# Branch projections: where the low parts of the streamed weights are computed, VectorE or GpSimd

## The chip, the cores and the metric

One core of a Trainium2 chip runs the whole program. The metric is the device time of one execution in microseconds (us), the median of several. TensorE, VectorE, ScalarE and GpSimd stand in the profile as PE, DVE, ACT and POOL, the queue that issues most transfers as SP; PEld is TensorE's loading of weights.

## The reference

One block of a transformer on 1024 tokens of width 1024, float32 throughout. Cut to what matters here:

```python
u = x * (1.0 + scale1) + shift1
proj = u @ w_in                       # 4808 columns: a_q a_k a_v b_q b_kv i_q i_k i_w gates
y_a = diff_attention(a_q, a_k, a_v)   # 4 heads x 2 maps, block-causal, ALiBi
score = sum_h i_w * relu(i_q . i_k)   # the indexer; the 256 best keys of a row are selected
o_lat = attention over the selected keys of c_kv, 8 heads
y_b = o_lat @ w_uv
mixed = sigmoid(gates_a) * (y_a @ w_a_proj) + sigmoid(gates_b) * (y_b @ w_b_proj)
x = layer_norm(alpha * x + gate1 * (mixed @ w_o))
# then 16 experts, two of them for each token, and a second layer norm
```

## The kernel before

Each float32 matrix that TensorE multiplies is split into a high part, the value rounded by ScalarE (`copy` in `halves`, L132), and a low part, the value less the high part (`sub`, L128). A product is then three matmuls, low by high, high by low and high by high (`mm3`, lines L142, L145, L146).

The streamed weights of the projections come in chunks of 128 columns: two transfers of 128x512 into `raw` (tag `wr`, two buffers), two copies into `wh` by ScalarE, two subtractions into `wl`. `wh` and `wl` have two buffers each, so the chunk after next is converted while TensorE works at the next. A chunk is 48 matmuls into `pj`. There are 34 chunks that go this way through `wload`: one of the indexer, one of `kv`, 12 of branch A, 4 of the queries of B, 16 of gates. `merge_a` multiplies the output of branch A by its merge weights, eight chunks of 128x512, which are split in the same way into halves of a `wab` buffer. Branch B's merge weights (`load_wab`), `w_o` and the experts' weights are split by the same function.

Two streams are woven by the generators' own numbers: `attentions` (scores of the indexer, the top-k search on VectorE, attention A, attention B) and `fillers` (`kv`, `b_keys`, gates, projections of A and B, `a_norm`, `merge_a`). The scheduler of the language then puts the instructions of each engine into one order by a model of their times; each engine, and each queue of transfers, works through its own order, and an instruction that waits holds everything behind it.

Names that the prediction uses. `ptr`, `pth`, `ptl`: the transposed probabilities and their two parts, which TensorE needs for `py` (attention A) and `pyb` (attention B). `plg`: logits, which VectorE takes out of PSUM as `P` at L762 and L778. `macc`: a sum over rows of the conditioning weights `adaw`, which VectorE makes in the middle of the projections (L694) from transfers of 512 KB, for values that are first needed behind the attentions; `gb` is read back from it. `yo` and `yq`: the output of attention A and its clipped copy (L900). `mask_d`: the masks that the top-k search ends in, stored from GpSimd's queue (L600) out of VectorE's `e` (L598). `bqq`, `bqh`, `bql`, `bv`: loads for a head of attention B, issued from GpSimd's queue (L263, L924). GpSimd does no arithmetic on tiles in this kernel: it fills constants, stores and loads.

Of the kernel before, what the change touches and what calls it, by code (L numbers as in the profile page):

```python
# [86 lines left out]
def block_kernel(ctx: ExitStack, tc, a, out):  # L87
    nc = tc.nc
    V, S, G, PE = nc.vector, nc.scalar, nc.gpsimd, nc.tensor
# [40 lines left out]
    def copy(o, i, e=None):  # L130
        if e is None:
            return S.activation(o, i, AF.Copy)  # L132
        return e.tensor_copy(o, i)
# [60 lines left out]
    def after(i, name):  # L194

        if name:
            tc.add_manual_dep(i.ins, name, mybir.DependencyInfo(mybir.DependencyClass.NoSync, mybir.DependencyReason.DATA),
                              reason="order of two streams")

    def halves(src, h, l, split, queue=dma, behind=None, tag="wr", raws=None, times=None):  # L200

        if raws is None:
            raws = fetch(src, h.shape[1], queue, tag)
        for c, raw in raws:
            cs = slice(c, c + raw.shape[1])
            if times is not None:
                V.tensor_tensor(raw, raw, times[:, cs], op=OP.mult)
            after(copy(h[:, cs], raw), behind)
            sub(l[:, cs], raw, h[:, cs], split)
        return h, l  # L210

    def fetch(src, n, queue, tag):
        w = 512 if tag in HALVES else 1024
        raws = []
        for c in range(0, n, w):
            raw = (s2 if tag in HALVES else s4)("raw", tag)[:, :min(w, n - c)]
            queue(raw, src[:, c:min(c + w, n)])
            raws.append((c, raw))
        return raws

    def wload(src, n=1024, split=V):
        return halves(src, s4("wh", "wh", dt=FR)[:, :n], s4("wl", "wl", dt=FR)[:, :n], split)

    def proj(ch, use, split=V, w=None, tag="mm"):

        h, l = w or wload(a["w_main"][ch], split=split)
        for half in range(2):
            p = bank("pj", tag)
            t = slice(half * 512, half * 512 + 512)
            for k in range(KC):  # L230
                c = slice(k * 128, k * 128 + 128)
                mm3(p, h[:, c], l[:, c], uh[k][:, t], ul[k][:, t], k == 0, k == KC - 1, True)
                if k % 2 and k < KC - 1:
                    yield 1.3
            use(half, p)
            for side, n in sides:
                for _ in range(n):
                    next(side, None)
            yield 1.3
# [83 lines left out]
    for n in range(3):  # L323
        tag = ("lg", "lg", "mm")[n]
# [700 lines left out]
    def merge_a():  # L1025
        for c in range(KC):
            w = s4("wab", ("wh", "wl")[c % 2], (128, 2, 512), FR)
            wh, wl = halves(a["w_ab"][c, :, 0:512], w[:, 0], w[:, 1], V, S.dma_start)
            for half in range(2):
                t = slice(half * 512, half * 512 + 512)  # L1030
                g = s2("gate", "sg")
                dma(g, gates_d[c, :, t])
                p = bank("pab", "mm")
                for k in range(4):
                    cs = slice(k * 128, k * 128 + 128)
                    mm3(p, wh[:, cs], wl[:, cs], yah[k][:, t], yal[k][:, t], k == 0, k == 3, True)
                    yield 2.5
                V.tensor_tensor(g, p, g, op=OP.mult)
                dma(gates_d[c, :, t], g)
# [71 lines left out]
    for c in range(KC):  # L1111
        wh, wl = wab.pop(0) if wab else load_wab(c)
# [719 lines left out]
```

## Time and profile before

| | us |
|---|---|
| median of 3 runs | 1384.12 (1382.36 to 1387.14) |
| the profiled execution | 1381.05 |
| its span, first to last instruction | 1379.2 |
| PE busy | 1255.9 (91%) |
| DVE busy | 977.6 (71%) |
| ACT busy | 682.6 (49%) |
| POOL busy | 122.4 (9%) |
[...]

The profiled execution took 1.85 us more than its span and lies 3.07 us under the median of the runs. Busy time is the union of an engine's instructions; matmuls overlap, so a stretch in which PE is busy all the time still has a pace of its own. Until about 640 us the projections run beside the top-k search and attention A, then attention B beside the merge of A until about 870 us; the output product, the routing and the experts follow, and the last norm ends the program.

### The profile page before, as it was taken

How to read it: one execution, taken by the hardware profiler on the slowest of the kernel's cores; microseconds unless marked ns; L12 is line 12 of the kernel's file. 1: busy time of each engine (PE TensorE's matmuls, PEld its weight loads, DVE VectorE, ACT ScalarE, POOL GpSimd, SP SyncE). 2: the span in 40 equal slices, each digit the busy share in tenths (PEclk: the TensorE clock that was granted, in tenths of full speed). 3: DMA queues.
4: the chain of work that ended last, by engine and by line, in shares of the span. 5: the costliest groups of instructions: out<-in, count | busy, mean ns of one | idle time of the engine just before them, and what ended most of it. 6: DMA issues, size and time to landing. Idle time of an engine off the chain costs nothing. (4 is left out here: it accounts for less than half of the span.)

```text
span 1379.2 us, 18485 instructions
## 1 busy us (share of the span) xinstructions
PE 1255.9 (91%) x6280; PEld 988.6 (72%) x6295; DVE 977.6 (71%) x2128; ACT 682.6 (49%) x1214; POOL 122.4 (9%) x154
## 2 busy tenths in 40 slices
PE   7999999999999999998889988899986989999950
PEld 6876778877777777666667777787865767788840
DVE  6547689783457758665676768888798889877736
ACT  4536662213785555445746556434224557554515
POOL 1000000000000001001001100000002222323120
PEclk9999999999999999999999998999996999999985
DMA  9211442123124317564445521675435788989856
GB/s 362 80 46 70 145 174 86 47 67 121 53 82 145 130 54 237 177 191 129 142 146 145 160 79 61 222 242 190 156 128 208 237 298 249 311 290 310 244 87 249
DMA packets 108485, 225.90 MB, mean 164 GB/s; under 512 B 33104, under 2 KB 39648, under 8 KB 108384
## 3 DMA queue, kind: packets, MB, share of 16 engines
q1 hardware_dynamic: 67952, 164.22, 33.8%
q0 software_dynamic: 35824, 52.03, 14.0%
q10 hardware_dynamic: 4608, 8.39, 1.9%
q8 instruction: 53, 0.87, 0.2%
q14 instruction: 48, 0.39, 0.1%
HBM read 169.94 MB, written 54.58 MB: 163 GB/s over the span
## 5 line engine op out<-in xcount | busy, mean ns | idle before, releaser
L142 PE MATMUL pj<-uh,wl 128*128 128x512 f32 x544 | 220.7, 406 | 1.6 <-ACT bkr L132 0.8
L145 PE MATMUL pj<-ul,wh 128*128 128x512 f32 x544 | 216.5, 398 | 0.0
L146 PE MATMUL pj<-uh,wh 128*128 128x512 f32 x544 | 215.9, 397 | 0.0
L128 DVE TENSOR_TENSOR ewl<-raw,ewh 128x1024 fp32r<-128x1024 f32 x102 | 122.2, 1218 | 28.6 <-ACT ewh L132 28.6
L132 ACT ACTIVATE ewh<-raw 128x1024 fp32r<-128x1024 f32 x102 | 105.6, 1057 | 61.5 <-DMA raw<-w_exp 61.0
L142 PEld LDWEIGHTS pj<-uh,wl 128*128 128x128 f32 x544 | 102.7, 189 | 35.1 <-issue 11.5
L146 PEld LDWEIGHTS pj<-uh,wh 128*128 128x128 f32 x544 | 102.5, 188 | 26.1 <-issue 5.6
L145 PEld LDWEIGHTS pj<-ul,wh 128*128 128x128 f32 x544 | 102.7, 189 | 23.6 <-issue 5.1
L132 ACT ACTIVATE pth<-ptr 128x512 fp32r<-128x512 f32 (+1 forms) x120 | 65.8, 552 | 70.8 <-PE ptr L793 39.0
L128 DVE TENSOR_TENSOR ptl<-ptr,pth 128x512 fp32r<-128x512 f32 (+1 forms) x120 | 75.4, 634 | 23.6 <-ACT pth L132 22.8
L142 PE MATMUL pgu<-ewh,xl 128*128 128x512 f32 x200 | 81.3, 407 | 0.0
L793 PE MATMUL ptr<-ident,P 128*128 128x128 f32 x432 | 72.8, 286 | 7.7 <-DVE ptl L128 6.4
L145 PE MATMUL pgu<-ewl,xh 128*128 128x512 f32 x200 | 79.0, 395 | 0.0
L146 PE MATMUL pgu<-ewh,xh 128*128 128x512 f32 x200 | 79.0, 395 | 0.0
L765 ACT ACTIVATE P<-P,mx 128x128 f32<-128x128 f32 (+7 forms) x64 | 49.4, 772 | 41.5 <-DVE mx L762 37.5
L1612 POOL DMA_INDIRECT acc_d<-ot,idxs x24 | 47.3, 1969 | 201.1 <-DVE ot L1611 133.0
L793 PEld LDWEIGHTS ptr<-ident,P 128*128 128x128 f32 x432 | 52.3, 147 | 15.9 <-DVE ptl L128 7.9
L128 DVE TENSOR_TENSOR wl<-raw,wh 128x512 fp32r<-128x512 f32 x68 | 44.9, 686 | 22.9 <-ACT wh L132 22.8
L780 ACT ACTIVATE P<-P,mx 128x128 f32<-128x128 f32 (+3 forms) x64 | 49.4, 773 | 21.7 <-DVE mx L778 20.4
L758 PE MATMUL plg<-ak,aq 64*128 64x512 f32 (+4 forms) x288 | 58.2, 375 | 0.6 <-DVE mx L762 0.6
L444 DVE SCALAR_TENSOR_TENSOR sc<-relu,iw,sc 128x512 f32<-128x512 f32 (+3 forms) x70 | 45.4, 653 | 17.9 <-ACT relu L439 16.0
L958 PE MATMUL pyb<-ptl,bv 128*128 128x256 f32 (+1 forms) x160 | 47.8, 322 | 7.1 <-DVE ptl L128 3.7
(443 smaller groups left out, 2966.6 us busy)
## 6 DMA issues: line engine op xcount, KB each, us to landing
raw<-w_exp SPq DMA_DIRECT2D x102, 512.0 KB
raw<-w_main SPq DMA_DIRECT2D x68, 256.0 KB
adaw<-ada_b SPq DMA_DIRECT2D x32, 512.0 KB
adaw<-ada_a SPq DMA_DIRECT2D x16, 512.0 KB
gates_d<-gt SPq DMA_DIRECT2D x32, 256.0 KB
gate<-gates_d SPq DMA_DIRECT2D x32, 256.0 KB
xt<-xT SPq DMA_DIRECT2D x8, 512.0 KB
bv_d<-bvs SPq DMA_DIRECT2D x16, 256.0 KB
```

What stands on the lines that cost most here:

```text
L128: e.tensor_tensor(o, i0, i1, op=OP.subtract)
L132: return S.activation(o, i, AF.Copy)
L142: i = PE.matmul(o, wl, xh, start=first, stop=False)
L145: PE.matmul(o, wh, xl, start=False, stop=False)
L146: e = PE.matmul(o, wh, xh, start=False, stop=last)
L444: V.scalar_tensor_tensor(acc, r[:, :n], w, acc, op0=OP.mult, op1=OP.add)
L758: i = PE.matmul(p[:, :n], q[a_][r, qs], k[b_][r, c0:c0 + n], start=m == 0, stop=m == 2)
L765: S.activation(P[:, :L], P[:, :L], AF.Exp, bias=mx_[:, 0:1], scale=-1.0, accum_out=mx_[:, 1:2])
L780: S.activation(P[:, :L], P[:, :L], AF.Exp, bias=mx[:, 0:1], scale=-1.0, accum_out=mx[:, 1:2])
L793: leads(PE.transpose(p[:, c:c + 128], Ps[s][:, kb * 128:kb * 128 + 128], ident))
L958: PE.matmul(y[:, c0:c0 + n], st, tl, start=kb == 0, stop=False)
L1612: where(cond_p and cond_p(), lambda: G.indirect_dma_start(out=acc_d, out_offset=bass.IndirectOffsetOnAxis(ap=isc, axis=0), in_=ot, in_offs ...
```

## The change

`wload` and `proj` take GpSimd as the engine of the subtraction unless told otherwise, and `merge_a` names it. High parts stay on ScalarE. `load_wab`, `load_wo`, the first four chunks and the experts name VectorE as before.

```diff
-    def wload(src, n=1024, split=V):
+    def wload(src, n=1024, split=G):
         return halves(src, s4("wh", "wh", dt=FR)[:, :n], s4("wl", "wl", dt=FR)[:, :n], split)
 
-    def proj(ch, use, split=V, w=None, tag="mm"):
+    def proj(ch, use, split=G, w=None, tag="mm"):
...
     def merge_a():
         for c in range(KC):
             w = s4("wab", ("wh", "wl")[c % 2], (128, 2, 512), FR)
-            wh, wl = halves(a["w_ab"][c, :, 0:512], w[:, 0], w[:, 1], V, S.dma_start)
+            wh, wl = halves(a["w_ab"][c, :, 0:512], w[:, 0], w[:, 1], G, S.dma_start)
```

That is 68 subtractions of 128x512 for the 34 chunks and 8 for `merge_a`. The scheduler orders all engines anew. Three places show it.

POOL, from the end of the constants to the first loads for attention B; `wl` rows are the moved subtractions, two for a chunk, and the six `mask_d` stores are the end of the top-k search. A line with + stands in the changed program alone.

```order
 L395 IOTA dtmp 128x1024
+L128 TENSOR_TENSOR wl<-raw,wh 128x512 x28
 L559 UNCONDITIONAL_BRANCH
+L128 TENSOR_TENSOR wl<-raw,wh 128x512 x2
 L600 DMA mask_d<-e_2973 128x384
 L600 DMA mask_d<-e_2995 128x512
 L600 DMA mask_d<-e_3018 128x640
+L128 TENSOR_TENSOR wl<-raw,wh 128x512 x2
 L600 DMA mask_d<-e_3056 128x768
 L600 DMA mask_d<-e_3092 128x896
 L747 MEMSET bias 64x64 x2
 L600 DMA mask_d<-e_3147 128x1024
```

Behind these rows come the two subtractions of the 17th chunk: they now stand behind the last mask store, and those of the 16th behind the third.

DVE, at the end of attention A, the last three sums over `adaw` and the first parts `ptl` of the transposed probabilities behind them. Before:

```order
L694 SCALAR_TENSOR_TENSOR macc_5785<-adaw_6197,cond_68,macc_5785 128x1024
L947 RECIPROCAL rden_711<-mx_6041 128x1
L947 RECIPROCAL rden_711<-mx_6100 128x1
L694 SCALAR_TENSOR_TENSOR macc_5785<-adaw_6200,cond_68,macc_5785 128x1024
L694 SCALAR_TENSOR_TENSOR macc_5785<-adaw_6325,cond_68,macc_5785 128x1024
L1146 TENSOR_SCALAR gb_9192<-gb_9192 128x8
L128 TENSOR_TENSOR ptl_5879<-ptr_5874,pth_5878 128x384
L128 TENSOR_TENSOR ptl_5997<-ptr_5991,pth_5996 128x512
L251 SCALAR_TENSOR_TENSOR hl_6192<-pj_6092,hl_6191 128x512
```

The same place in the changed program:

```order
L128 TENSOR_TENSOR ptl_5879<-ptr_5874,pth_5878 128x384
L947 RECIPROCAL rden_711<-mx_6100 128x1
L128 TENSOR_TENSOR ptl_5997<-ptr_5991,pth_5996 128x512
L694 SCALAR_TENSOR_TENSOR macc_5785<-adaw_6197,cond_68,macc_5785 128x1024
L1146 TENSOR_SCALAR gb_9192<-gb_9192 128x8
L694 SCALAR_TENSOR_TENSOR macc_5785<-adaw_6200,cond_68,macc_5785 128x1024
L251 SCALAR_TENSOR_TENSOR hl_6192<-pj_6092,hl_6191 128x512
L694 SCALAR_TENSOR_TENSOR macc_5785<-adaw_6325,cond_68,macc_5785 128x1024
L900 TENSOR_SCALAR yq_5957<-yo_5954 128x256
L128 TENSOR_TENSOR ptl_6012<-ptr_6006,pth_6011 128x512
```

Two `ptl` have moved ahead of the three sums; `yq_5957` and `ptl_6012` stay behind them. ACT at the same time, before, where `raw` waits for a buffer that a `wl` subtraction frees:

```order
L132 ACTIVATE wh_6468<-raw_6472 128x512
L217 DMA raw_6917<-w_ab 128x512
L217 DMA raw_7083<-w_ab 128x512
L132 ACTIVATE yo_5954<-py_5833 128x256
L132 ACTIVATE pth_6011<-ptr_6006 128x512
```

And in the changed program:

```order
L132 ACTIVATE wh_6468<-raw_6472 128x512
L132 ACTIVATE yo_5954<-py_5833 128x256
L132 ACTIVATE pth_6011<-ptr_6006 128x512
L901 ACTIVATE yq_5957<-yq_5957 128x256
L217 DMA raw_6917<-w_ab 128x512
L217 DMA raw_7083<-w_ab 128x512
```

The two transfers have moved behind `yo`, `pth` and `yq`.

DVE, early in attention B, the third and fourth chunk of `merge_a` ahead of two reads of logits. Before:

```order
L128 TENSOR_TENSOR ptl_6389<-ptr_6383,pth_6388 128x512
L128 TENSOR_TENSOR wab_7486<-raw_7487,wab_7486 128x512
L128 TENSOR_TENSOR wab_7296<-raw_7297,wab_7296 128x512
L778 ISA P_6501,mx_6502<-plg_6503,bias_6352 128x512
L778 ISA mx_6502 128x1
L778 ISA P_6516,mx_6517<-plg_6518,bias_6352 128x320
```

The same place in the changed program:

```order
L128 TENSOR_TENSOR ptl_6389<-ptr_6383,pth_6388 128x512
L778 ISA P_6501,mx_6502<-plg_6503,bias_6352 128x512
L778 ISA mx_6502 128x1
L778 ISA P_6516,mx_6517<-plg_6518,bias_6352 128x320
L778 ISA mx_6517 128x1
```

The two `wab` rows are gone from DVE; TensorE's order at this place is the same in both programs.

## Rows read from the trace of the kernel before

**Rows 1.** The page: busy time of an engine, its share, instructions.

```profile
PE 1255.9 (91%) x6280; PEld 988.6 (72%) x6295; DVE 977.6 (71%) x2128; ACT 682.6 (49%) x1214; POOL 122.4 (9%) x154
```

**Rows 2.** Windows: stretch, length, busy us of PE, PEld, DVE, ACT, POOL; clock; DMA.

```profile
68.00:540.00 472.00, 469.42 (x2263) 356.65 (x2261) 317.87 (x755) 239.63 (x450) 6.16 (x14) 1.00 0.29 100
187.00:316.00 129.00, 127.49 (x564) 103.36 (x563) 110.52 (x257) 35.14 (x64) 3.79 (x8) 1.00 0.28 96
540.00:640.00 100.00, 93.83 (x471) 68.66 (x470) 61.31 (x151) 45.33 (x94) 6.82 (x10) 0.97 0.61 181
640.00:815.00 175.00, 158.72 (x898) 124.07 (x909) 119.43 (x329) 106.93 (x213) 15.81 (x26) 0.97 0.48 140
815.00:935.00 120.00, 109.36 (x547) 88.56 (x548) 96.89 (x202) 54.58 (x103) 0.82 (x2) 0.96 0.50 168
```

**Rows 3.** Line L128's subtractions and L444: shortest, median, longest ns; first, last start.

```profile
L128 DVE TENSOR_TENSOR wl<-raw,wh x68: 667/685/694, 67.7 to 625.5; 128x512 fp32r<-128x512 f32 x68
L128 DVE TENSOR_TENSOR wab<-raw,wab x16: 662/684/693, 641.3 to 895.5; 128x512 fp32r<-128x512 f32 x16
L444 DVE SCALAR_TENSOR_TENSOR sc<-relu,iw,sc x70: 467/671/753, 88.2 to 189.0; 128x512 f32<-128x512 f32 x35, 128x384 f32<-128x384 f32 x14, 128x320 f32<-128x320 f32 x14, 128x256 f32<-128x256 f32 x7
```

**Rows 4.** Groups on POOL: count, busy us, mean ns, idle before.

```profile
L1423 POOL MEMSET zt<- 128x512 f32 x1 | 0.5, 540 | 6.9 <-DVE mxl L128 6.9
L395 POOL IOTA dtmp<- 128x1024 f32 x1 | 1.0, 994 | 28.5 <-DVE mod L351 28.5
```

**Rows 5.** Timeline by engine, 291 to 316 us: start, duration, instruction, idle before.

```profile
299.81 0.69 DVE L128 TENSOR_TENSOR wl<-raw,wh 128x512 fp32r<-128x512 f32 x1
300.19 0.54 POOL L600 DMA_DIRECT2D mask_d<-e  x1 [4.60 <-DVE e L598]
303.03 0.39 PE L142 MATMUL pj<-uh,wl 128*128 128x512 f32 x1
305.14 0.63 ACT L132 ACTIVATE wh<-raw 128x512 fp32r<-128x512 f32 x1 [0.79 <-DMA raw<-w_main]
314.44 0.50 PE L142 MATMUL pj<-uh,wl 128*128 128x512 f32 x1 [0.36 <-ACT gt L720]
314.89 0.54 POOL L600 DMA_DIRECT2D mask_d<-e  x1 [0.78 <-DVE e L598]
```

**Rows 6.** Timeline by engine, 619 to 628 us.

```profile
619.14 1.28 DVE L694 SCALAR_TENSOR_TENSOR macc<-adaw,cond,macc 128x1024 f32<-128x1024 f32 x1 [4.32 <-DMA adaw<-ada_b]
621.98 1.28 DVE L694 SCALAR_TENSOR_TENSOR macc<-adaw,cond,macc 128x1024 f32<-128x1024 f32 x1 [1.56 <-DMA adaw<-ada_b]
623.26 1.15 DVE L128 TENSOR_TENSOR ptl<-ptr,pth 128x384 fp32r<-128x384 f32 x2
623.86 0.58 PE L145 MATMUL py<-ptl,avh 128*128 128x256 f32 x1 [4.72 <-DVE ptl L128]
625.63 1.05 ACTq L217 DMA_DIRECT2D raw<-w_ab  x2
626.79 0.38 ACT L132 ACTIVATE yo<-py 128x256 f32<-128x256 f32 x1 [10.20 <-DVE wl L128]
627.21 0.29 DVE L900 TENSOR_SCALAR yq<-yo 128x256 f32<-128x256 f32 x1 [1.00 <-ACT yo L132]
```

**Rows 7.** Timeline by engine, 667 to 670 us.

```profile
667.75 0.97 ACT L132 ACTIVATE pth<-ptr 128x512 fp32r<-128x512 f32 x2
667.89 0.69 DVE L128 TENSOR_TENSOR wab<-raw,wab 128x512 fp32r<-128x512 f32 x1 [1.73 <-ACT wab L132]
668.50 0.68 DVE L778 CUSTOM_DVE_ANT_0 P<-plg,bias 128x512 f32<-128x512 f32 x1
669.24 0.79 PE L774 MATMUL plg<-bql,bqq 128*128 128x512 f32 x1 [2.31 <-DVE mx L778]
```

**Rows 8.** Windows, with the granted clock behind the six busy columns.

```profile
621.40:628.20 6.80, 4.34 (x15) 3.85 (x16) 5.02 (x9) 1.39 (x4) 0.70 (x2) 0.50 0.74 217
669.10:672.50 3.40, 3.26 (x11) 2.55 (x13) 2.19 (x9) 2.90 (x5) 0.00 (x0) 0.51 0.49 158
```

## Prediction

> **What bounds the kernel now.** I read the page first: TensorE is busy for 91% of the span, VectorE for 71%, GpSimd for 9% [rows 1]. An average over stages decides nothing, so the windows come next [rows 2]. Between 68 and 540 us, where 30 of the 34 projection chunks are converted and the whole top-k search lies, TensorE is busy 469.4 of 472.0 us at the full granted clock. Every microsecond that VectorE gains there is worth nothing, unless TensorE waits for VectorE, and it does not. From 540 on TensorE idles: 6.2 us up to 640, 16.3 us up to 815 and 10.6 us up to 935, 33 us in all, and the clock falls below 1.00. Only there can work taken off VectorE shorten the program. So the question is which of those waits end at one of the moved instructions, or at something queued behind one.
>
> **What is moved.** 68 subtractions `wl` at 685 ns (46.6 us) and the first 8 of the 16 `wab` rows at 684 ns (5.5 us) leave VectorE [rows 3]. The same 76 go to GpSimd, which so far does no such instruction in this trace. Its price p has to be bounded: below by the fill of a tile of the same 128x512, 0.54 us, one pass that only writes; above by three such passes one after the other, two reads and a write, 1.6 us [rows 4]. I take two passes, 1.1 us, because two operands must come in. [...]
>
> **Term 1, the slower subtraction itself: 0.** Each chunk's `wl` is needed when TensorE has finished the chunk before it, and the double buffer leaves time. The shortest two gaps of the 34 are those of the 16th and 17th chunk: the 16th is ready at 300.50 and first used at 303.03, 2.5 us later [rows 5]; all but these two have 5 us or more. Two subtractions cost 2.2 us in place of 1.4 us, 0.8 us more; at 1.6 us, 1.9 us more. Both fit even into the 2.5 us. And those two chunks are late today only because VectorE is in the top-k search: ScalarE had done its half of the 17th at 305.8, 8.7 us ahead of the first use at 314.44 [rows 5]. If that cover were gone, each chunk that comes late costs TensorE what it is late by.
>
> **Term 2, GpSimd's queue: 0, with a condition.** GpSimd now holds the two subtractions of the 17th chunk behind the last mask store, which was issued at 314.89, after the first use of that chunk at 314.44 [rows 5]. Were VectorE no faster than today, the chunk would be ready at 314.89 + 0.54 + 2 x 1.1 = 317.6 and TensorE would wait 3.2 us. But VectorE is busy 110.5 of 129 us between 187 and 316 [rows 2], and 22 of the moved subtractions lie in that stretch ahead of the last store, 15 us by 685 ns each. If the search gains more than 3.2 of those 15 us, the wait is nil. I take nil. The loads and fills for attention B behind other `wl` rows in that queue wait for TensorE anyway, and the subtractions ahead of them have their data by then.
>
> **Term 3, the wait at 619 us: -4 us.** Here VectorE stood behind three sums `macc` whose transfers came late (4.32 us and 1.56 us of waiting in the two that are shown); the `ptl` that TensorE needed came behind them at 623.26, and TensorE idled 4.72 us [rows 6]. ScalarE was held too, for 10.2 us, since its transfer of `w_ab` waited for a `wl` on VectorE behind the same sums. In the new order two `ptl` stand ahead of the sums, and ScalarE's `yo` and `pth` ahead of that transfer. What still stands behind the sums is `yq` and the next `ptl`. With transfers as late as now, the last sum ends at 623.26; 0.29 us for `yq` and 0.69 us for `ptl` give 624.2. TensorE gets there later than 619.1: from the first `ptl` on it has 37 matmuls to do, and it reaches that `ptl` 15 matmuls earlier, both counted in TensorE's new order. At the mean pace of 68 to 540 us (472 us for 2263 matmuls, 0.21 us each [rows 2]) that is 619.1 - 3.2 + 7.8 = 623.7; many of the 37 are half as wide, so it may be 622. The wait left is 0.5 to 2.2 us, and 2.5 to 4.2 us are gained, 3.3 in the middle. Behind the wait the clock stood at half for 6.8 us, of which some 4.3 us were worked in, so 2.2 us were lost to it [rows 8]; a wait of half the length may still cost the shorter fall of 3.4 us [rows 8]. I add 0.7 us.
>
> **Term 4, the wait at 669 us: -2.5 us.** VectorE waits 1.73 us for ScalarE's half of a `wab`, subtracts for 0.69 us, and only then reads the logits at 668.50; TensorE, which needs that PSUM bank, idles 2.31 us [rows 7]. In the new order VectorE goes from a `ptl` straight to the logits. The next `ptl` still needs ScalarE's `pth` of 667.75, so some 1.1 us of the wait may come back one step later. The gain is 1.2 to 2.3 us, and 3.4 us at half clock behind it, worth 1.7 us [rows 8], may go. Between 1.2 and 4.0 I take 2.5.
>
> **Term 5, the other six `wab` subtractions, 717 to 761 us: -0.5 us.** They stand among `ptl` rows at 0.6 to 0.7 us each, and no wait of TensorE over 0.5 us follows one directly.
>
> **The sum.** 0 + 0 - 4 - 2.5 - 0.5 = -7 us. The profiled execution took 1381.05 us, so 1374 us in its measure; it lies 3.07 us under the median of the runs, so **1377 us** as a median, 0.5% less.
>
> **Rivals.** *A. Nothing to see.* All orders are new from the first scores on, and 33 us of small waits on long chains behind 540 us can come out elsewhere: what `yq` loses behind `macc`, for example, is the same 4.72 us one step on if the transfers land 3 us later. Against it speaks that TensorE's order in attention B is unchanged where term 4 lies. It gives 1381 to 1387 us.
>
> *B. Slower, through VectorE being held up.* If a VectorE instruction that takes both inputs from SBUF could not run beside a GpSimd subtraction, VectorE would pay for what it gave away. The indexer's sums (70 at some 0.67 us, 88 to 189 us [rows 3]) and the end of the search are of this kind, while `ptl` and the logits take one input from PSUM. The place is the last mask store, the price is that of the 17th chunk. With 22 subtractions of 1.1 us each holding VectorE fully, 24.2 us come back for the 15 us saved; the last store falls to about 324, the chunk is ready at 326.9, and TensorE waits 12.4 us in place of none, plus some 2 us of clock. Less the 7 us above, that is +7: 1391 us. TensorE begins to wait when VectorE loses more than 11.8 of its 15 us; from 18.8 us on the wait outweighs the gains. For it speaks that VectorE is nearly full in that stretch [rows 2]; against it that most of the search's time is one-input counting. [...] No row of the trace shows it, since GpSimd reads no tile so far; at full strength in that stretch it would make the 1391 us.
>
> *C. More than forecast.* VectorE's relief shortens further links of attention B's chain: a third of the 33 us of idling in place of the fifth or so above, with its clock: 1370 us.
>
> **Chances.** Forecast 0.43, C 0.13, A 0.28, B 0.16. 0.3%, about what a measurement of this kernel tells from no change, is 4.2 us. Forecast and C are faster, but the forecast's near end (-4) is not: faster 0.54, same 0.29, slower 0.17. The range takes in C and part of B, from 1368 to 1389 us. Its low end is C with 2 us to spare, its high end B less the last 2 us; the forecast alone would be 1373 to 1381.
>
> **What would show it.** Right: POOL subtractions at about 1.1 us; TensorE still full from 68 to 540 us; first uses of the 16th and 17th chunk without a wait; the idle 4.72 us at 619 cut to 2 us or less; the 2.31 us at 669 cut to about 1 us; the chain from 935 us on as before, only earlier. Wrong: TensorE waiting for `wl` on POOL at about 314 us, or VectorE instructions of L444 and L594 to L597 longer than now (B); the same sum of TensorE's idle time behind 540 us in other places (A). A price of 4 us or more on GpSimd would break term 1 in the whole search.

## The result, and the profile after the change

The changed kernel is slower. Its median is 1396.0 us (1391.7 to 1403.0, 8 runs), beside 1384.6 us (1375.3 to 1393.6, 8 runs) for the kernel before: a ratio of 1.010, 95% interval 1.0072 to 1.0128. Timed once more beside other kernels it gave 1.0077 (1.0048 to 1.0106). The profiled execution took 1393.96 us, 12.9 us more than that of before, and its span is 1391.9 us, at a mean granted clock of TensorE of 0.955 (0.958 before).

The page's first part (busy time of an engine, its share of the span, instructions), against [rows 1]:

```profile
PE 1259.5 (90%) x6280; PEld 992.2 (71%) x6295; DVE 958.2 (69%) x2052; ACT 680.3 (49%) x1214; POOL 225.2 (16%) x230
```

GpSimd took on 102.8 us of work. VectorE was to get 52.1 us lighter (46.6 us of `wl`, 5.5 us of `wab`); its busy time fell by only 19.4 us. Where the rest went shows in the lines L128, L444 and L694 (shortest, median and longest ns, first and last start), against [rows 3]:

```profile
L128 POOL TENSOR_TENSOR wl<-raw,wh x68: 1267/1294/2369, 67.1 to 632.0; 128x512 fp32r<-128x512 f32 x68
L128 POOL TENSOR_TENSOR wab<-raw,wab x8: 1272/1286/1327, 647.5 to 764.1; 128x512 fp32r<-128x512 f32 x8
L444 DVE SCALAR_TENSOR_TENSOR sc<-relu,iw,sc x70: 470/744/1591, 87.9 to 190.0; 128x512 f32<-128x512 f32 x35, 128x384 f32<-128x384 f32 x14, 128x320 f32<-128x320 f32 x14, 128x256 f32<-128x256 f32 x7
L694 DVE SCALAR_TENSOR_TENSOR macc<-adaw,cond,macc x28: 1265/1284/4192, 435.1 to 629.6; 128x1024 f32<-128x1024 f32 x28
```

A subtraction takes 1.29 us on GpSimd, and up to 2.37 us where VectorE is in its way (at 535.74 us, beside a `macc` that starts 0.05 us ahead of it and takes 1.27 us). L444's longest grew from 753 ns [rows 3] to 1591 ns, and one `macc` took 4.19 us. Of all VectorE instructions, 28 are over 0.1 us longer than the longest of their kind before, 24.0 us together, and 20 of the 28 lie up to 320 us. The timeline by engine shows how one comes about:

```profile
238.49 2.55 POOL L128 TENSOR_TENSOR wl<-raw,wh 128x512 fp32r<-128x512 f32 x2 [8.84 <-ACT wh L132]
238.51 1.29 DVE L518 SCALAR_TENSOR_TENSOR dt<-dt 128x6 f32<-128x6 f32 x1
240.15 0.92 DVE L519 TENSOR_TENSOR dt<-dt,dc 128x6 f32<-128x6 f32 x1
```

L518 works on 6 columns and took at most 163 ns before. Here it starts 0.02 us behind a GpSimd subtraction and ends with it, 1.29 us later; L519 does the same beside the second one. Neither row shows a wait ahead of it: the time runs from the instruction's own start to its end. I call this a hold. Held are instructions with two SBUF inputs (longest here, and longest of the kind before: L444 1591 and 753 ns, L694 4192 and 1286, L597 1426 and 1015, L882 1168 and 163) and one-input tensor-scalars (L592 1796 and 682, L900 1349 and 481, L530 1275 and 168). Beside subtractions lie also 6 `ptl` and 24 reads of logits, which take one input from PSUM, and 7 of the search's counts in L487, a tensor-scalar that also writes its accumulator; none of these is held, and none is more than 2 ns longer than the longest of its kind before.

The windows, against [rows 2] (length, busy us of PE, PEld, DVE, ACT, POOL, clock, DMA):

```profile
68.00:540.00 472.00, 466.21 (x2248) 353.58 (x2247) 300.56 (x693) 239.48 (x451) 85.52 (x73) 1.00 0.28 96
187.00:316.00 129.00, 124.07 (x546) 99.79 (x545) 110.60 (x237) 35.23 (x65) 31.23 (x29) 1.00 0.27 91
540.00:640.00 100.00, 92.99 (x451) 68.30 (x450) 61.36 (x139) 41.96 (x89) 17.07 (x18) 0.95 0.65 201
640.00:815.00 175.00, 156.80 (x888) 123.18 (x899) 113.28 (x316) 104.49 (x209) 27.86 (x36) 0.97 0.48 137
815.00:935.00 120.00, 110.53 (x563) 90.33 (x565) 93.48 (x199) 55.82 (x108) 0.27 (x1) 0.94 0.44 149
```

The second window tells most. In the search VectorE is busy 110.60 us, as before (110.52), with 20 instructions fewer: all that it gave away came back as holds. And TensorE, which idled 1.5 us there, now idles 4.9 us. Behind 540 us, where the forecast saw something to gain, it idles 34.7 us up to 935 us instead of 33.1.

To see where time is lost I took the start of each TensorE matmul in this trace less its start in the trace of before, and call that its lateness. It is 2.0 us from 110 us on, 5.4 us at 335, 4.7 at 680, 7.9 at 830, 11.9 at 975 and 12.9 at the end. The two steps up to 335 us, in the timeline by engine, first in before and then after the change:

```profile
96.86 1.48 PE L433 MATMUL psc<-ik,iq 64*128 64x384 f32 x9
103.81 0.97 PE L433 MATMUL psc<-ik,iq 64*128 64x512 f32 x6
296.72 0.68 DVE L128 TENSOR_TENSOR ak<-pj,ak 128x512 fp32r<-128x512 f32 x1
301.34 0.68 DVE L592 TENSOR_SCALAR eq<-sc,ktval 128x896 bf16<-128x896 f32 x1
```

```profile
96.19 0.78 PE L433 MATMUL psc<-ik,iq 64*128 64x384 f32 x3
96.91 0.49 PE L146 MATMUL pj<-uh,wh 128*128 128x512 f32 x1
97.33 0.97 PE L433 MATMUL psc<-ik,iq 64*128 64x512 f32 x3
98.90 0.96 PE L433 MATMUL psc<-ik,iq 64*128 64x512 f32 x3
295.45 0.47 PE L142 MATMUL pj<-uh,wl 128*128 128x512 f32 x1 [1.23 <-DVE ak L128]
300.35 1.80 DVE L592 TENSOR_SCALAR eq<-sc,ktval 128x896 bf16<-128x896 f32 x1
300.37 2.91 POOL L128 TENSOR_TENSOR wl<-raw,wh 128x512 fp32r<-128x512 f32 x2
302.07 0.68 DVE L128 TENSOR_TENSOR ak<-pj,ak 128x512 fp32r<-128x512 f32 x1
302.80 0.50 PE L142 MATMUL pj<-uh,wl 128*128 128x512 f32 x1 [1.65 <-DVE ak L128]
```

The first step, 2.0 us, has no wait of TensorE in it, and the clock is full in both traces (1.00 in the first window). The new order parts what ran side by side. A `psc`, a matmul of the scores, uses 64 of TensorE's 128 rows (64*128 above, where a `pj` is 128*128), and in a longer row of them two can start together: the six at 103.81 us started in pairs 0.01 us apart and took 0.97 us, where three by themselves take 0.96. From 96 us on, 18 of them stood in three groups before, nine, three and six, 3.41 us together. Now they stand in six groups of three with projections `pj` between them, and take 5.60 us: 2.2 us more. No run changes this order alone, so it is a reading of the trace.

The second step, 3.4 us, is waits. TensorE does not wait for a `wl`. It waits for VectorE to clear a projection out of PSUM (`ak`), and in the last wait `ak` stands in VectorE's queue behind L592, held 1.1 us. Two things come together here. The last mask store goes out at 314.8 us, where it went out at 314.89 before [rows 5]: the search gained nothing. And VectorE's new order puts `ak` further back: this one stood ahead of the L592 of 896 columns before (296.72 and 301.34 us) and now stands behind it (302.07 and 300.35 us), four rows later, which took 3.8 us together before. No run parts the two in the changed kernel.

The later steps are smaller and mixed. From 335 to 680 us the lateness falls by 0.7 us on balance. At 790 us it rises by 3.2 us (1.8 us more idle and 1.7 us of clock), at 940 us by 3.5 us (1.4 and 1.7 us), and the rest is 1 to 2 us in small pieces.

The wait of [rows 6] has moved one step and grown:

```profile
623.47 1.28 DVE L694 SCALAR_TENSOR_TENSOR macc<-adaw,cond,macc 128x1024 f32<-128x1024 f32 x1 [3.37 <-DMA adaw<-ada_b]
629.63 1.27 DVE L694 SCALAR_TENSOR_TENSOR macc<-adaw,cond,macc 128x1024 f32<-128x1024 f32 x1
630.24 3.05 POOL L128 TENSOR_TENSOR wl<-raw,wh 128x512 fp32r<-128x512 f32 x2
630.82 1.35 DVE L900 TENSOR_SCALAR yq<-yo 128x256 f32<-128x256 f32 x1
632.67 1.01 PE L611 MATMUL prms<-one_f,yq 128*128 128x1 f32 x4 [5.60 <-ACT yq L901]
```

The sums still wait for `adaw`, the last one starts at 629.63 instead of 621.98, `yq` behind it is held 0.9 us by the 34th chunk's subtraction, and TensorE idles 5.60 us instead of 4.72. Earlier, behind the held `macc` of 4.19 us, TensorE also idles 1.03 us at 555.33 for logits (L762) that VectorE takes up late. The wait of [rows 7] (2.31 us) has turned into two, 1.09 us for a `ptl` and 0.57 us at its old place:

```profile
668.26 0.39 PE L958 MATMUL pyb<-ptl,bv 128*128 128x256 f32 x1 [1.09 <-DVE ptl L128]
674.42 0.50 PE L774 MATMUL plg<-bql,bqq 128*128 128x512 f32 x1 [0.57 <-DVE mx L778]
```

The lateness falls there from 6.9 us at 664 to 4.7 us at 682.

### The profile page after: what moved, and what is told of

Same layout as the page of the kernel before. It is cut to its first block, busy times and chain, and to the rows that moved or that the text cites. A ratio compares the mean times of both kernels' runs of the same rounds, so it can differ in the third digit from the quotient of the medians.

```text
span 1391.9 us, 18518 instructions
## 1 busy us (share of the span) xinstructions
PE 1259.5 (90%) x6280; PEld 992.2 (71%) x6295; DVE 958.2 (69%) x2052; ACT 680.3 (49%) x1214; POOL 225.2 (16%) x230
## 4 chain that ended last, share of the span: by engine, by line
PE 35%; DMA 24%; DVE 8%; issue 8%; ACT 3%; POOLq 0%; POOL 0%; DVEq 0%; SPq 0%; another core or an unknown queue 0%; ACTq 0%
DMA acc_d<-ot,idxs 13%; PE pj L142 5%; PE pj L145 4%; PE pj L146 4%; PE plg L758 3%; DMA adaw<-ada_b 3%; PE ptr L793 3%; DMA raw<-w_o 2%; PE po L142 2%; PE po L145 2%; PE po L146 2%; DMA gates_d<-gate 1%; PE pyb L958 1%; DMA ya<-ya_d 1%; DVE macc L694 1%
## 5 line engine op out<-in xcount | busy, mean ns | idle before, releaser
L128 POOL TENSOR_TENSOR wl<-raw,wh 128x512 fp32r<-128x512 f32 x68 | 92.0, 1372 | 389.0 <-ACT wh L132 361.0
L128 DVE TENSOR_TENSOR ewl<-raw,ewh 128x1024 fp32r<-128x1024 f32 x102 | 122.5, 1219 | 32.6 <-ACT ewh L132 32.4
L142 PEld LDWEIGHTS pj<-uh,wl 128*128 128x128 f32 x544 | 102.8, 189 | 38.1 <-issue 14.7
L145 PEld LDWEIGHTS pj<-ul,wh 128*128 128x128 f32 x544 | 102.9, 189 | 24.6 <-issue 6.1
L128 DVE TENSOR_TENSOR ptl<-ptr,pth 128x512 fp32r<-128x512 f32 (+1 forms) x120 | 75.6, 633 | 28.1 <-ACT pth L132 27.1
L444 DVE SCALAR_TENSOR_TENSOR sc<-relu,iw,sc 128x512 f32<-128x512 f32 (+3 forms) x70 | 50.1, 719 | 24.6 <-ACT relu L439 22.0
L762 DVE CUSTOM_DVE_ANT_0 P<-plg,bias 128x512 f32<-128x512 f32 (+4 forms) x64 | 34.7, 560 | 46.4 <-PE plg L758 45.1
L780 ACT ACTIVATE P<-P,mx 128x384 f32<-128x384 f32 (+4 forms) x64 | 49.3, 772 | 21.8 <-DVE mx L778 21.3
```

The costliest lines, as they stand in the source:

```text
L128: e.tensor_tensor(o, i0, i1, op=OP.subtract)
L142: i = PE.matmul(o, wl, xh, start=first, stop=False)
L145: PE.matmul(o, wh, xl, start=False, stop=False)
L444: V.scalar_tensor_tensor(acc, r[:, :n], w, acc, op0=OP.mult, op1=OP.add)
L762: V.tensor_tensor_reduce(P[:, c0:c0 + n], p[:, :n], bias[:, c0:c0 + n], 1.0, mx_[:, 5:6] if n_ else 3.0e38, OP.add, OP.min, mx_[:, 0:1] if ...
L780: S.activation(P[:, :L], P[:, :L], AF.Exp, bias=mx[:, 0:1], scale=-1.0, accum_out=mx[:, 1:2])
```

## The experiments

Theory H: a GpSimd subtraction holds VectorE instructions, and the loss is where VectorE sets TensorE's pace. Rivals: O, the loss is in the new order behind 640 us; L, low parts come too late; Q, GpSimd's queue. Chunks are numbered 1 to 34 in program order. All times together (before was timed beside each group; held: count and sum of instructions over 0.1 us longer than the longest of their kind in before; the last three columns: TensorE's lateness in the profiled execution at 335, 680 and 975 us of before's time). The lateness holds what a trace begins with: at 60 us, before any moved subtraction has run, it lies between -1.0 and 1.1 us, and at -2.9 us in e9.

| kernel | subtractions on GpSimd | median us | ratio to before, 95% | held | at 335 | at 680 | at 975 |
|---|---|---|---|---|---|---|---|
| the change | all 76 | 1396.0 | 1.010 (1.0072 to 1.0128) | 28, 24.0 us | 5.4 | 4.7 | 11.9 |
| e1 | 34 chunks | 1389.6 | 1.0033 (1.0009 to 1.0056) | 27, 23.9 us | 6.0 | 10.5 | 11.3 |
| e2 | merge of A | 1384.0 | 1.0013 (0.9989 to 1.0037) | 1, 1.1 us | -0.1 | -1.6 | 3.6 |
| e3 | chunks 1 to 17 | 1387.7 | 1.0024 (0.9992 to 1.0056) | 20, 16.1 us | 6.3 | 4.7 | 2.8 |
| e4 | chunks 18 to 34 | 1381.8 | 0.9995 (0.9966 to 1.0023) | 8, 7.9 us | -0.7 | 1.9 | 0.4 |
| e5 | all 76, again | 1393.8 | 1.0077 (1.0048 to 1.0106) | 28, 24.0 us | 5.3 | 4.9 | 11.5 |
| e6 | 68 more, none moved | 1392.0 | 1.0053 (1.0016 to 1.0090) | 36, 29.9 us | 5.9 | 5.8 | 6.0 |
| e7 | 68 copies more | 1382.4 | 0.9999 (0.9969 to 1.0029) | 24, 7.6 us | 1.7 | 1.2 | 1.5 |
| e8 | 68 fills more | 1389.2 | 1.0037 (1.0004 to 1.0069) | 2, 0.5 us | 0.5 | 4.1 | 5.1 |
| e9 | all 76, mask by SyncE | 1390.5 | 1.0055 (1.0027 to 1.0082) | 28, 24.6 us | 5.7 | 4.0 | 9.9 |
| e10 | chunks 18 to 34, merge | 1388.3 | 1.0032 (1.0006 to 1.0058) | 8, 7.9 us | 0.3 | -0.5 | 2.3 |
| e11 | all, in halves | 1394.1 | 1.0084 (1.0051 to 1.0117) | 47, 18.5 us | 6.1 | 5.7 | 12.4 |
| e12 | chunks 18 to 29 | 1377.5 | 0.9969 (0.9941 to 0.9996) | 4, 3.0 us | -1.0 | -5.3 | -8.4 |
| e13 | chunk 34 | 1389.2 | 1.0014 (0.9989 to 1.0039) | 0 | 0.5 | -0.2 | 3.8 |
| e14 | chunks 18 to 33 | 1386.0 | 0.9997 (0.9971 to 1.0022) | 7, 7.0 us | 0.6 | 4.1 | 2.2 |
| e15 | chunks 30 to 33 | 1387.9 | 0.9993 (0.9965 to 1.0022) | 3, 4.7 us | 1.1 | 1.4 | 1.8 |
| e16 | chunks 18 to 29, again | 1383.0 | 0.9960 (0.9934 to 0.9986) | 5, 3.1 us | -0.7 | -5.5 | -4.2 |

### Which part loses: e1 to e4, e10, e5

e1 and e2 take one of the two edits each; e3, e4 and e10 choose by a counter, as here for e3:

```diff
+    nth = [0]
     def wload(src, n=1024, split=V):
+        nth[0] += 1
+        split = G if nth[0] <= 17 else V
```

e1: 

> The projections' 68 subtractions on GpSimd, branch A's merge weights back on VectorE. Theory H (a GpSimd subtraction holds up a VectorE instruction that reads its inputs from SBUF until the subtraction ends, and VectorE sets the pace in the scores, the search and at a few places behind them): all 22 us of lengthening are beside these 68, so the time stays 10 to 13 us above before, near 1395. Theory O (the loss comes from the new order of VectorE, GpSimd and DMA instructions behind 640 us, around the merges of branch A): half the loss or more goes with the merges, 1385 to 1390.

e2: 

> Only the 8 subtractions of branch A's merge weights on GpSimd, the projections on VectorE. Theory H: no VectorE instruction was found lengthened beside these 8, so the time is within 3 us of before, 1382 to 1387, or a little under it. Theory O: 4 to 8 us slower than before, 1389 to 1393.

e3: 

> GpSimd subtracts for the first 17 of the 34 chunks (scores and search, up to 320 us), VectorE for the rest and for the merges. Theory H: the loss that the trace shows by 320 us stays, 5.4 us, so 1388 to 1392; VectorE lengthened by some 14 us in all. Theory O: nothing, 1383 to 1386, since all that is left behind 320 us is as before.

e4: 

> GpSimd subtracts for the last 17 of the 34 chunks (branch A's attention, from 320 us on), VectorE for the first 17 and for the merges. Theory H: VectorE waits for TensorE most of this stretch, so its 8 us of lengthening there cost 1 to 4 us, 1385 to 1389, and this with the loss of the first 17 makes up that of all 68. Theory O: as slow as the change or nearly, 1390 to 1396, since the order behind 540 us is the changed one.

e5: 

> The change itself once more, to stand beside the others on one chip: before is 1384, the projections alone took 1390 and the merges alone 1384. Theory H (held-up VectorE instructions): the merges add nothing, so some 1390 to 1392, and the 1396 of the first measurement was partly chance. Theory I (projections and merges on GpSimd together cost more than the two apart, by the order that the scheduler gives them): 1394 to 1398 again.

e10: 

> GpSimd subtracts for the last 17 chunks and for branch A's merge weights; the first 17 chunks are back on VectorE. Theory H: the 5 us lost up to 320 us are gone, and what is left is that of the last 17 and the merges by themselves (0 and 0.4 us), so 1383 to 1387. Theory I (projections and merges together cost 4 to 6 us by the order behind 640 us): 1389 to 1393.

With the first 17 chunks on GpSimd, TensorE is 5.3 to 6.3 us late at 335 us in every kernel, and without them no more than 1.1 us, unless GpSimd does extra work: the loss up to there is theirs. Some 2 us of it are the new order of the scores (above), which all six of these kernels share, the rest the search. The last 17 lose nothing that can be measured, nor do the merges by themselves (e2). But H's number for e1 was too high: about 5 us, not 10 to 13, and e1's 1389.6 us lies in O's range. In e3 the 6.3 us of the trace are 3 to 4 us in the medians, a little under H's range, and their interval still holds 1; the trace's lateness is down to 4.7 us at 680 and 2.8 at 975. e4's 1381.8 us is below both ranges.

The parts do not quite add up. e1 and e2 make 0.46%, e3 and e10 make 0.56%; the whole was 1.0% and 0.77%. Each of these has an interval of 0.2 to 0.4% to either side, so most of the difference may be chance. e5's 1393.8 us lies just under I's range and above H's (1390 to 1392), e10's 1388.3 us in neither. One place where the merges cost is shown by e2, in the timeline by engine:

```profile
791.37 0.43 DVE L133 COPY rr<-rden 128x512 f32<-128x512 f32 x1 [6.04 <-DMA gates_d<-gate]
792.18 0.58 PE L958 MATMUL pyb<-ptl,bv 128*128 128x256 f32 x1 [3.97 <-DVE yb L962]
```

VectorE's `rr` waits for a store of `gates_d` to free its buffer, and TensorE behind it. This TensorE wait is 3.6 to 4.0 us in all six kernels with the merges on GpSimd, and 2.2 us or less in before and in the eleven others. In e2 the lateness rises there from -1.8 to 1.4 us, which uses up what the merges had gained at 669 us. Why the store lands later wasn't tried.

### The hold by itself: e6, e7, e8

VectorE keeps all its subtractions; GpSimd does one thing more behind each, which nobody reads (e6 below; e7 has `G.tensor_copy(raw, raw)`, e8 `G.memset(raw, 0.0)` in its place):

```diff
-            sub(l[:, cs], raw, h[:, cs], split)
+            sub(l[:, cs], raw, h[:, cs], split); more and sub(raw, raw, h[:, cs], G)
```

e6: 

> The kernel before, with VectorE's 68 subtractions of the projections where they were, and behind each one a second subtraction of the same size on GpSimd whose result nothing reads (it goes over the raw tile, which is then free 1.3 us later). Nothing is moved off VectorE. Theory H: VectorE's instructions with two inputs in SBUF get 10 to 25 us longer in all, up to 1.3 us for one of 0.16 us, and the time is 3 to 12 us above before. Theory L (the loss came from low parts that are later and from the order, not from a hold-up): VectorE's durations as before, time within 3 us of before.

e7: 

> As the run with a second subtraction, but GpSimd copies the raw tile onto itself: one input from SBUF instead of two. If any read of SBUF by GpSimd holds VectorE up (theory H, wide): VectorE's two-input instructions are lengthened here too, by up to one duration of the copy. If it takes GpSimd's two inputs (theory H, narrow): no VectorE instruction is over 0.1 us longer than before, and the time is before's within 3 us.

e8: 

> The control: GpSimd fills the raw tile with zeros, with no input at all. Theory H: an instruction of GpSimd that reads nothing from SBUF does not hold up a VectorE instruction with two SBUF inputs, so their durations are as before, and the time is within 3 us of before. If GpSimd's mere activity on SBUF counts, VectorE's instructions are lengthened by up to 0.5 us (a fill of 128x512 takes 0.54 us in the trace of before).

The same instructions of the search in the three traces, by the timeline (L520 took 0.16 us before). e6:

```profile
203.69 2.94 POOL L128 TENSOR_TENSOR raw<-raw,wh 128x512 f32<-128x512 f32 x2 [11.91 <-DVE dt L519]
204.15 1.26 DVE L520 TENSOR_TENSOR dt<-dt,ktop 128x6 f32<-128x6 f32 x1
314.82 2.29 DVE L596 SCALAR_TENSOR_TENSOR e<-cs,kneed,eq 128x1024 bf16<-128x1024 f32 x1
317.14 1.06 ACT L746 ACTIVATE bias<-dist 128x1024 f32<-128x1024 uint16 x1 [2.64 <-DVE e L596]
318.74 0.50 PE L142 MATMUL pj<-uh,wl 128*128 128x512 f32 x1 [3.46 <-ACT gt L720]
```

e7:

```profile
204.32 1.59 POOL L209 COPY raw<-raw 128x512 f32<-128x512 f32 x2 [13.07 <-DVE dt L519]
204.80 0.58 DVE L520 TENSOR_TENSOR dt<-dt,ktop 128x6 f32<-128x6 f32 x1
```

e8:

```profile
202.81 0.53 POOL L209 MEMSET raw<- 128x512 f32 x1 [12.38 <-DVE dt L519]
203.30 0.16 DVE L520 TENSOR_TENSOR dt<-dt,ktop 128x6 f32<-128x6 f32 x1
203.49 0.53 POOL L209 MEMSET raw<- 128x512 f32 x1 [0.15 <-DVE dt L520]
203.49 0.17 DVE L521 TENSOR_TENSOR g<-dt,klow 128x6 f32<-128x6 f32 x1
```

L520 takes 1.26 us beside a subtraction (median 1.29 in the change) and 0.58 beside a copy (median 0.65). In e8 it meets only the last 0.04 us of a fill and takes 0.16 us; L521 behind it starts with the next fill and takes 0.17 us, where it took 1.21 in e6 and 0.52 in e7. So one SBUF input of GpSimd was enough (e7: H wide), a fill that reads nothing did not hold these two, and the shorter instruction held for less. In e6 nothing was taken off VectorE and TensorE's order in this stretch is that of before, and TensorE is 5.9 us late at 335 us. From 187 us on it loses 6.1 us, of which 4.8 are idle time and 1.7 clock, less some small gains. The two large waits hang on held instructions of VectorE. At 195 us (2.27 us) TensorE waits for ScalarE's `gt`, and ScalarE for a store whose values VectorE wrote late, behind a sum of L444 held to 1.78 us. At 319 us (3.46 us) it waits for a `gt` that stands behind ScalarE's `bias`, which waited 2.64 us for VectorE's `e`, held to 2.29 us and 4.3 us late. So holds, with TensorE's order unchanged and no wait for a low part, make TensorE lose that much: neither L nor O. They do it at other waits than the change's, which loses 3.3 us between 187 and 335 us; e6 shows what holds can do, not which wait they make in the change. H fails in most of the scores: nine sums of L444 are held in e6, up to 1.78 us, and TensorE is 0.2 us early at 180 us. The holds sum to 29.9 us, above H's 10 to 25. e7's 7.6 us of holds cost 1 us by 335 us (0.7 of the 1.7 us are there from the start) and nothing in the time. In e8 two VectorE tensor-scalars were held, 0.5 us in all (L523 took 0.47 us for 0.16), so a fill is not quite free of it. e8's 1389 us is above what was expected; its trace is level with before up to 560 us and then gets 3.7 us late at one place, where TensorE waits 1.35 us for VectorE and the clock behind it stands at 0.50 for 6.8 us (the window, columns as above):

```profile
568.00:574.80 6.80, 6.80 (x21) 5.12 (x20) 5.53 (x17) 4.46 (x10) 1.05 (x2) 0.50 0.36 136
```

Other kernels have that wait (1.0 to 2.0 us); full clock follows it in e2, e3, e6, e9 and e13, a fall in e1, e4, e10, e11 and e14. I have no cause for it from the fills. The interval nearly reaches 1, and a ratio of 1.0037 that nothing explains is a measure for the other small ratios of the table.

### The queue and the size of a piece: e9, e11

e9 issues the mask stores by `dma(...)` on SyncE instead of `G.dma_start(...)`; e11 cuts each subtraction on GpSimd into two of 128x256.

e9: 

> The change with the search's mask stores issued from SyncE instead of GpSimd, so that no subtraction stands behind a store that waits for the search. Theory Q (the queue of GpSimd, term 2 of the prediction, costs the time in the search): the sixteenth chunk's subtraction starts near 295.5 us instead of 300.4, the two TensorE waits at 295 and 303 us (1.2 and 1.6 us) go, and the time falls by 3 us or more against the change, to 1387 to 1391. Theory H (held-up VectorE instructions): the subtraction starts earlier, but both waits end on a VectorE instruction that is late because of its own lengthened ones, so they stay within 0.5 us and the time is the change's, 1391 to 1396.

e11: 

> The change with GpSimd's subtractions cut into halves of 128x256, 152 of some 0.65 to 0.75 us instead of 76 of 1.29. Theory H with a hold for one whole instruction of GpSimd: a VectorE instruction of 0.16 us takes at most 0.9 us instead of 1.3, the lengthening falls from 24 us to 10 to 17, and the time by 2 to 5 us against the change, 1388 to 1392. If the two engines share the way to SBUF piece by piece instead: the lengthening stays at 22 to 26 us, and the time at 1393 to 1396.

e9, timeline by engine:

```profile
293.96 0.47 PE L142 MATMUL pj<-uh,wl 128*128 128x512 f32 x1 [1.23 <-DVE ak L128]
293.96 3.56 POOL L128 TENSOR_TENSOR wl<-raw,wh 128x512 fp32r<-128x512 f32 x2 [9.30 <-ACT wh L132]
302.26 0.50 PE L142 MATMUL pj<-uh,wl 128*128 128x512 f32 x1 [2.58 <-DVE ak L128]
```

The 16th chunk's subtraction starts at 294.0 instead of 300.4 us, and both waits are still there, the second longer (2.58 us for 1.65): Q falls. From 60 to 335 us this trace loses 8.6 us and the change's 5.2. Still, its 1390.5 us would fit Q and is a little below H's range, and the second wait grew by more than the 0.5 us that H allowed.

e11, timeline by engine:

```profile
239.06 2.83 POOL L128 TENSOR_TENSOR wl<-raw,wh 128x256 fp32r<-128x256 f32 x4 [8.55 <-ACT wh L132]
240.10 0.42 DVE L519 TENSOR_TENSOR dt<-dt,dc 128x6 f32<-128x6 f32 x1
240.56 0.66 DVE L520 TENSOR_TENSOR dt<-dt,ktop 128x6 f32<-128x6 f32 x1
```

The hold of a small VectorE instruction goes with one instruction of GpSimd: held ones now take up to 0.73 us, beside pieces of some 0.71 us (2.83 us for the four above), not 1.29. But there are 47 holds instead of 28, which I put down to an instruction that got past one piece and meets the next; the sum fell only to 18.5 us, and the time not at all. H's sum (10 to 17 us) and its 1388 to 1392 us were wrong there; the 1394.1 us lies in the other theory's range, the sum in neither.

### The wait behind macc, and a version that is faster: e12 to e16

These use the same counter, with `17 < len(nth) < 30`, `len(nth) == 34`, `17 < len(nth) < 34` and `29 < len(nth) < 34`, and the merges on VectorE.

e12: 

> GpSimd subtracts for chunks 18 to 29 alone (branch A's attention up to 540 us, where VectorE waits for TensorE most of the time); the others, and the merges, on VectorE. Theory H: three to five VectorE instructions lengthened, 3 to 5 us in all, none of them waited for; 0 to 2 us below before, 1382 to 1384, which a measurement of this kernel can't tell from it. If relief of VectorE were worth anything to TensorE there: 3 us or more below before, 1381 or less, and this version would beat both kernels.

e13: 

> GpSimd subtracts for the 34th chunk alone; TensorE's order is then that of before to the last row, and VectorE's too but for the two rows taken out, which stand behind the late macc and behind the ptl that TensorE waits for. Term 3 of the prediction in its simplest form (VectorE is relieved behind macc, so TensorE waits less near 619 us): 2 to 4 us below before. Theory W (that wait is set by the arrival of adaw, and rows behind the awaited ptl can't shorten it): 4.0 to 5.0 us of waiting stay and the time is before's within 2 us, 1382 to 1386.

e14: 

> GpSimd subtracts for chunks 18 to 33, not for the 34th. Chunks 18 to 29 alone took 6 us less than before and chunks 18 to 34 took 2 us less. Theory M (chunks 30 to 33 meet the macc sums at 540 to 560 us, hold one of them for 4.2 us, and move the late chain of adaw and macc back): 1381 to 1386, as with all 17, with one macc of 3 to 4.2 us and a TensorE wait of 5 us or more near 620 to 630 us. Theory L (it is the 34th chunk that undoes the gain): 1376 to 1380.

e15: 

> GpSimd subtracts for chunks 30 to 33 alone. Theory M: one macc near 550 us takes 3 to 4.2 us instead of 1.28, and the time is 1 to 4 us above before, 1385 to 1388. Theory L: no loss, 1380 to 1385.

e16: 

> Chunks 18 to 29 on GpSimd once more, since the first measurement gave a ratio of 0.997 with an interval that ends just below 1. If the gain is real: 1376 to 1381, a ratio of 0.995 to 0.998, with the TensorE wait near 619 us at 3 us or less instead of 4.72. If it was chance: 1382 to 1385.

e13, timeline by engine, in TensorE's order of before:

```profile
623.98 0.38 PE L145 MATMUL py<-ptl,avh 128*128 128x256 f32 x1 [3.95 <-DVE ptl L128]
937.98 0.50 PE L142 MATMUL po<-woh,mxl 128*128 128x512 f32 x1 [3.44 <-DVE r L1210]
```

The wait at 619 us stays (3.95 us): the relieved rows stand behind the `ptl` that TensorE awaits. This is theory W, though the wait came out 0.05 us under its range, the time 3 us over it, and the interval holds 1. The second row is a warning: here, 300 us behind the only edit, TensorE idles 3.44 us where before it idled 2.02, because a transfer of `xr` landed later; the clock behind it is lower too (0.65 for 4 us, where it was full), and the lateness rises from 0.1 to 3.8 us. A step like this one, at 940 us, is in most of the traces (3.5 us in the change's, 5 in e5's); a single profile can't put it down to the change.

e14, timeline by engine, and below it e15 and e16:

```profile
546.05 4.19 DVE L694 SCALAR_TENSOR_TENSOR macc<-adaw,cond,macc 128x1024 f32<-128x1024 f32 x1
546.62 2.52 POOL L128 TENSOR_TENSOR wl<-raw,wh 128x512 fp32r<-128x512 f32 x2
```

```profile
546.03 4.13 DVE L694 SCALAR_TENSOR_TENSOR macc<-adaw,cond,macc 128x1024 f32<-128x1024 f32 x1
624.94 0.58 PE L145 MATMUL py<-ptl,avh 128*128 128x256 f32 x1 [7.11 <-DVE ptl L128]
```

```profile
543.91 1.28 DVE L694 SCALAR_TENSOR_TENSOR macc<-adaw,cond,macc 128x1024 f32<-128x1024 f32 x1
612.53 0.39 PE L145 MATMUL py<-ptl,avh 128*128 128x256 f32 x1 [1.76 <-DVE ptl L128]
618.43 1.28 DVE L694 SCALAR_TENSOR_TENSOR macc<-adaw,cond,macc 128x1024 f32<-128x1024 f32 x1 [0.48 <-DMA adaw<-ada_b]
```

With chunks 30 to 33 one `macc` takes 4.1 to 4.2 us, in e14, in e15 and in the change alike. Without them (e16) none is held there, the last one starts at 618.4 us instead of 622.0, and TensorE waits 1.76 and 1.39 us in place of 4.72. From e16 to e14 the last `macc` goes from 618.4 to 628.5 us and the lateness at 680 us from -5.5 to 4.1 us: it is chunks 30 to 33, not the 34th, that undo the gain (M, not L). That the held `macc` is how they do it is not shown. e15 has the same hold and its last `macc` starts at 623.1 us, 1.1 us later than before; its TensorE wait is long (7.11 us) because TensorE gets there earlier, and its time is level with before (0.9993, with an interval up to 1.0022, so M's price of 1 to 4 us is neither shown nor excluded). In e14 the TensorE waits stay under 3 us, where M wanted 5 or more.

The shorter wait is not what e12 and e16 gained either. Between 335 and 660 us of before's time they need 4.2 and 4.8 us less for the same matmuls, but TensorE's idle time there is before's within 0.4 us, and so is what the clock takes. The new order of TensorE is quicker: it goes from one kind of matmul to another 333 times where it did 349 times before, and more matmuls start side by side (163 and 165 against 155). In e14 (346 changes) the same stretch costs 3.5 us more, from idle time (1.5 us) and clock (5.1 us), while its order saves 3.1. So what chunks 18 to 29 bring is an order that the scheduler happened to find; which part of it comes from VectorE's relief, no run separates.

e12 and e16, the same kernel, are 0.31% and 0.40% below before, both intervals below 1, though e16's median of 1383.0 us lies in the range given for chance. H had said 0 to 2 us; it was 4 to 6 us here, where few VectorE instructions are held (3 us in all) and none that TensorE waits for. e8's unexplained 0.37% the other way is a reason for care with gains of this size.

## Why the prediction was wrong

The forecast was 1377 us and faster; the range ended at 1389 us, and the time was 1396 us. The sum said -7 us for the profiled execution, and 12.9 came. By the lateness they are: 2.2 us in the scores, 3.3 in the search (187 to 335 us), 0.9 up to 640, -1.5 up to 682, 3.2 at 790, 0.5 up to 925, 3.5 at 940 and 1.0 to the end (-0.2 stands at the start). By the prediction's steps:

- **What bounds the kernel: half right.** "Every microsecond that VectorE gains there is worth nothing" came out in the search. But a TensorE that is busy all the time can still gain or lose by its own order, and that had no term: the scores took 2 us more in the changed order, and with chunks 18 to 29 alone the stretch up to 660 us took 4 to 5 us less (e12, e16). Nor was the other side priced: such a TensorE lost where VectorE came late. With the first 17 chunks on GpSimd it was 6.3 us late by 335 us (e3).
- **The price p: off by 0.2 us.** 1.29 us, inside the bounds 0.54 to 1.6, against 1.1 taken.
- **Term 1: right.** No TensorE wait ends at a `wl`; the closest, the 17th chunk, is ready 2.0 us ahead of its use.
- **Term 2: this is the step that failed.** The queue costs nothing (e9), but the 0 hung on the search gaining more than 3.2 of its 15 us. It gained 0.1 us, since holds gave back what VectorE had saved, and TensorE lost 3.3 us between 187 and 335 us. The 17th chunk comes in time only because TensorE is itself late, by `ak`, which VectorE's order had moved back behind four rows of that search.
- **Term 3: wrong sign.** -4 us was forecast, 0.9 us were lost between 335 and 640 us; TensorE waits 5.60 us, not 4.72. "With transfers as late as now" failed: the last sum starts 7.7 us later. Rival A's remark, that `yq` loses the same wait one step on, was right. Moving only the rows of the 34th chunk does nothing (e13). Where chunks 30 to 33 stay on VectorE (e16) the wait is shorter (1.76 us), and a gain of the forecast's size is there, but through TensorE's order and not through the wait.
- **Term 4: right in size.** 2.31 us became 1.09 and 0.57 us, the first the residue of 1.1 us that was named; the lateness falls by 2.2 us there, against 2.5 forecast, and with the merges alone TensorE is 1.6 us early at 680 us.
- **Term 5: missed.** -0.5 us was forecast, and 3.2 us were lost. It looked only for waits that follow one of the six rows directly; 30 us further on TensorE waits 3.68 us in place of 1.53 (3.97 in e2).
- **Rival B: the right mechanism, and given 0.16.** The hold is there at full length. Its place was wrong: not the 17th chunk behind the last mask store, but VectorE's eviction `ak` ahead of it. Its price was too high (3.3 us in the search, not 12.4, since VectorE lost about what it saved there), and it left out what the new order costs in the scores and at the merges. The argument against it, that counting is most of the search's time, was true: L487 was not held (at most 1280 ns, as before), but the short instructions between were.

Shown: the loss by 335 us comes with the first 17 chunks (e3); a GpSimd subtraction by itself, with nothing moved, makes TensorE lose 6.1 us in the search (e6), though at other waits; the longer `macc` chain comes with chunks 30 to 33 (e14, e16). Read from the trace only: the 2 us of the scores' order, which the parted `psc` account for. Not separated: in the change's search, the holds and VectorE's new place for `ak`; as I read the trace both were needed, since the search gained nothing and `ak` stood behind more of it. Open: 3 to 7 us of the median. The parts sum to 0.5%, the whole is 0.8 to 1.0%, which the intervals leave room for as chance; the `gates_d` wait belongs to the merges, and the step at 940 us appears in e13 without a cause in the edit.

## What to carry to other kernels

The work moved from VectorE to GpSimd, which reads SBUF for it, was not gone from VectorE here: 52.1 us left it, and its busy time fell by 19.4 us. So count the VectorE instructions that will lie beside the moved work and take two SBUF inputs or are one-input tensor-scalars, and charge each up to one GpSimd instruction, small ones too (1.13 us for L518's 128x6 values here; a `macc` here: two, 2.9 us). The `ptl`, the logits and L487's counting, beside the same subtractions, were at most 2 ns over the longest of before; so move it to stretches where VectorE waits and works from PSUM, and keep it away from a chain that a transfer hangs on; here 12 chunks of 34 gained 0.3 to 0.4% where the whole change lost about 1%. A full TensorE at full clock says that relief shortens no wait. It doesn't say that delay costs nothing (3.3 us between 187 and 335 us here), nor that a new order of its own matmuls does (2.2 us in the scores); compare TensorE's order in both programs before putting a term at 0.

## What the runs showed of the hardware

- Of VectorE's instructions on 128x6 values, one went from 0.16 to 1.29 us beside a GpSimd subtraction (L518, the change), one from 0.16 to 0.58 beside a copy (L520, e7), and one stayed at 0.17 beside a fill (L521, e8, where two tensor-scalars were held, 0.5 us in all).
- Two GpSimd subtractions back to back held one `macc` through both: 4.13 to 4.19 us for 1.28 us (the change, e14, e15). A `macc` of 4.17 to 4.20 us is in e4, e5, e9 and e10 too, all with chunks 30 to 33 on GpSimd in whole pieces. The hold went the other way too, up to 2.37 us for a subtraction of 1.29 us (the change).
- Halving GpSimd's instructions raised the count of holds from 28 to 47 and cut their sum by a quarter only, from 24.0 to 18.5 us (e11).
- Matmuls that use 64 of TensorE's 128 rows ran side by side: six in a row took 0.97 us (before), three 0.96 (the change), and 18 of them 3.41 us in three groups (before) and 5.60 us in six (the change).
